# Pooling pass: where ScalarE's joining copy of two widths stands in its queue

## The chip, the cores and the metric

One core of a Trainium2 chip runs the whole program. The metric is device time in microseconds (us) of one execution; lower is better. The core's engines run side by side, each through its own list of instructions in the order in which it was written: PE multiplies matrices into banks of PSUM, DVE (VectorE) and ACT (ScalarE) do element-wise work and copy results out of the banks, POOL (GpSimd) does a little more of the same, and SP issues the DMA transfers. They wait for one another on semaphores.

## What is computed

A token encoder layer: normalise, one input projection, three mixers side by side (A: a gated MLP over chunks of 128 positions, B: pooling, C: a Fourier transform), each with a SiLU gate, one output projection, and a normalised residual. The change is in mixer B, which cuts to this:

```python
POOL_WINDOWS = (2, 4, 8, 16)
for g, w in enumerate(POOL_WINDOWS):          # four groups of 96 channels
    lo = jnp.clip(pos - w // 2, 0, s)
    hi = jnp.clip(pos + w // 2, 0, s)
    mean = (cs[:, hi] - cs[:, lo]) / (hi - lo)  # cs: running sum over positions
    outs.append(mean - zf[..., sl])
yb = mixer_b(b_in, b_w, b_scale) * jax.nn.silu(b_gate)
```

The inputs are two sequences of 4096 and 2048 positions, 1024 channels wide, in fp32.

## The kernel before

The kernel goes through the 6144 positions several times. The pass that matters here (about 485 to 950 us of the execution) computes mixer B's input z and its gate g for six blocks of 1024 positions; a pass of the same form for mixer A follows it. Each block is two halves h = 0, 1 of 512 positions (TB), and 384 channels are three tiles t = 0, 1, 2 of 128 rows. Because four pooling widths of 96 channels lie on three tiles of 128 rows, every tile holds rows of two widths.

**Products and slots.** Each block's projection is done with seven products instead of eight (a Strassen-like scheme), in the order P1, X1, P2, X2, Y1, X3, Y2 (`WIDE["b"]`). One product is one `slot` call. A slot runs its product three times, once for each t (twelve groups of matmuls of 128x512, three for each of four k, L141 to L143, 36 in all), and between them come the other engines' steps: `fill_a` before the copy out of the first bank, `fill_b` before the second, then `beside()`, which does one step of the Fourier mixer. The third bank's copy is put off to the start of the next slot (`tail`). Also at the start of a slot the operand of the next product is cut into a high part (ACT, L137) and a low part (DVE, L138). P1, X1, X2 and X3 accumulate in one bank per tile: P1 is copied out (ACT, L1337, into z), X1's matmuls then add onto the same bank, which is copied out again (L1339), and so on. So X1's first matmul on tile t waits until P1's copy of tile t is done. X2 (L1343) and X3 (L1347) are copied out by ACT too; P2 (L1341), Y1 (L1345) and Y2 (L1349) are added out by DVE.

**Pooling.** `pool_means` takes one tile of z and forms sums of 2, 4, 8, 16 neighbours by adding shifted slices on DVE (L1230 to L1243): tile 0 ends in `b` on rows 96 up, tile 1 in `b` on all rows, tile 2 in `c`. The last addition writes the wider window's rows into `a`; the rows of the narrower window are joined into `a` by one ACT copy, `nc.scalar.copy(a[rows, to], src[rows, to])` (L1245). Then, after the first `yield`, DVE scales and subtracts z on all rows (L1250). `sums(h, t)` runs a tile up to the first yield, `means(h, t)` the rest. `silu(h)` is three ACT activations (L1289), each followed by a copy of 8 columns; `gate(h)` is three DVE products (L1311) and puts three stores on the list for SP.

**Where the six joins of a block stand.** The slots' lists `fa` (fill_a) and `fb` (fill_b) say it: (0,0) in slot X2's fill_a, (0,1) in its fill_b, (0,2) in Y1's fill_a, (1,0) in Y2's fill_a, (1,1) in its fill_b, and (1,2) in fill_a of the next block's P1, where the next block's `new_z` (three copies of 16 columns, L1276) comes ahead of it and `means(1,1)` and `silu(0)` behind it. The last block's (1,2) stands in the same place of the first slot of mixer A's pass, whose P1 is copied out by ACT at L1483. `close_sequence` runs `pool_means` with n = 8 for the end of a sequence. All this is under a hand-written schedule: each engine runs its instructions in the order in which the program writes them.

Of the kernel before, what the change touches and what calls it, by code (L numbers as in the profile page):

```python
# [18 lines left out]
TB = 512  # L19
# [14 lines left out]
def hybrid_encoder(  # L34
# [33 lines left out]
    nc = tc.nc  # L68
# [209 lines left out]
    def ftile(name, shape, dt=F32):  # L278
        return fpool.tile(list(shape), dt, tag="f", name=name, bufs=7)
# [50 lines left out]
    def add_rest(sq, eng):  # L330
        eng.tensor_add(sq[0], sq[0], sq[2])
        eng.tensor_add(sq[0][:, 0:HB], sq[0][:, 0:HB], sq[0][:, HB : 2 * HB])
        return sq[0]

    def sum_rows(name, halves):

        n = 2 * len(halves)
        ps = bank(f"pss{name}", (P, NCH))[:, :n]
        for c in range(n):
            lh = halves[c // 2][:, (c % 2) * P : (c % 2) * P + P]  # L340
            nc.tensor.matmul(ps[:, c : c + 1], lh, ones[:, 0:1], start=True, stop=True)
        return ps
# [276 lines left out]
    with tc.manual_schedule(engines={E.PE, E.DVE, E.Activation, E.Pool}):  # L619
# [3 lines left out]
        rows = sum_rows("00", [add_rest(sqa, V)])  # L623
# [28 lines left out]
        rows = sum_rows("01", [add_rest(sqb, V)])  # L652
# [168 lines left out]
    def load_operand(j):  # L821
        if j < len(todo):
            n, b, m = todo[j]
            lo = lp[j % 3].tile([P, 2, 4, HB], F32R, tag="l", name=f"{n}{b}_{m}l")
            for h in range(2):
                nc.sync.dma_start(
                    lo[:, h].bitcast(F32).rearrange("p k t -> p (k t)"), op_d[2 * b + h, OUT_ORDER.index(m)]
                )
            whole[j] = lo

    def cut_operand(j):

        if j < len(todo):
            n, b, m = todo[j]
            lo = whole.pop(j)
            hi = hp[j % 2].tile([P, 2, 4, HB], F32R, tag="h", name=f"{n}{b}_{m}h")
            for h in range(2):
                split(lo[:, h].bitcast(F32), hi[:, h], lo[:, h])
            cut[j] = hi, lo
# [26 lines left out]
    def part(i, what):  # L866
        if 0 <= i < len(steps) and getattr(steps[i], what):
            getattr(steps[i], what)()

    def beside():  # L870
        i = at[0]
        if i <= len(steps) + 1:
            part(i - 2, "store")
            part(i + 2, "load")
            part(i, "compute")
            part(i + 2, "pre")
            at[0] += 1
# [279 lines left out]
            steps.extend(transform_steps(s, pair))  # L1157


    stores, tail = [], []  # L1160

    def flush(lst):
        fs, lst[:] = lst[:], []
        for f in fs:
            f()

    def slot(j, pairs, evict, fill_a=(), fill_b=(), loads=(), then=None, cuts=(), late=False, fill_c=(), more=0):


        m = todo[j][2]  # L1170
        load_operand(j + 2)
        if not late:
            flush(stores)
        for f in loads:
            f()
        flush(tail)
        cut_operand(j + 1)
        op = cut.pop(j)
        ps = pairs[0].product(m, op)
        for f in fill_a:  # L1180
            f()
        evict(0, ps)
        if late:
            done, stores[:] = stores[:late], stores[late:]
            flush(done)
        beside()
        ps = pairs[1].product(m, op)
        for f in cuts:
            f()
        for f in fill_b:  # L1190
            f()
        evict(1, ps)
        beside()
        for f in fill_c:
            f()
        last = pairs[2].product(m, op)
        for _ in range(more):
            beside()
        if then:
            then()  # L1200
        tail.append(lambda: evict(2, last))
# [17 lines left out]
    def pool_means(z, n, t, name, corr_at=None):  # L1219


        V = nc.vector

        def tile_(x, tag, bufs):
            if n < TB:
                return ftile(f"p{x}{name}", (P, n + 16))
            return e1.tile([P, TB + 16], F32, tag=tag, name=f"p{x}{name}", bufs=bufs)

        a, b = tile_("a", "a", 6), tile_("b", "w", 2)
        V.tensor_add(a[:, 1 : n + 16], z[:, 0 : n + 15], z[:, 1 : n + 16])  # L1230
        to = slice(8, n + 8)
        if t == 0:
            V.tensor_add(b[96:, to], a[96:, 7 : n + 7], a[96:, 9 : n + 9])  # L1233
            rows, src = slice(96, P), b
        else:
            V.tensor_add(b[:, 2 : n + 15], a[:, 1 : n + 14], a[:, 3 : n + 16])
            if t == 1:
                V.tensor_add(a[64:, to], b[64:, 6 : n + 6], b[64:, 10 : n + 10])
                rows, src = slice(0, 64), b
            else:  # L1240
                c = tile_("c", "w", 2)
                V.tensor_add(c[:, 4 : n + 13], b[:, 2 : n + 11], b[:, 6 : n + 15])
                V.tensor_add(a[0:96, to], c[0:96, 4 : n + 4], c[0:96, 12 : n + 12])  # L1243
                rows, src = slice(96, P), c
        nc.scalar.copy(a[rows, to], src[rows, to])  # L1245
        yield a
        if corr_at is not None:
            k, src = corr_at
            V.tensor_mul(a[:, k : k + 8], a[:, k : k + 8], corr_sb[:, 16 * t + src : 16 * t + src + 8])
        V.scalar_tensor_tensor(a[:, to], a[:, to], invw[t], z[:, to], ALU.mult, ALU.subtract)  # L1250
        yield a

    class PoolBlock:
# [41 lines left out]
        def sums(self, h, t):  # L1295
            self.half[h, t] = pool_means(
                self.z[h][t], TB, t, f"{self.b}_{h}_{t}", (16, 0) if self.t0 == 0 and h == 0 else None
            )
            next(self.half[h, t])
# [34 lines left out]
        def evict(self, m, t, ps):  # L1334
            z, g = self.z, self.g
            if m == "P1":
                nc.scalar.copy(z[0][t][:, 16:], ps)  # L1337
            elif m == "X1":
                nc.scalar.copy(g[0][t][:, 8:], ps)  # L1339
            elif m == "P2":  # L1340
                nc.vector.tensor_add(z[0][t][:, 16:], ps, z[0][t][:, 16:])  # L1341
            elif m == "X2":
                nc.scalar.copy(g[1][t][:, 8:], ps)  # L1343
            elif m == "Y1":
                nc.vector.tensor_add(g[1][t][:, 8:], ps, g[1][t][:, 8:])  # L1345
            elif m == "X3":
                nc.scalar.copy(z[1][t][:, 16:], ps)  # L1347
            else:
                nc.vector.tensor_add(g[0][t][:, 8:], ps, g[0][t][:, 8:])  # L1349

    before = None
    for b in range(NB // 2):
        blk = PoolBlock(b)
        pairs = [Wide(t, f"b{b}_{t}") for t in range(3)]
        p = before
        means = lambda who, h, t: lambda: who.means(h, t)
        sums = lambda who, h, t: lambda: who.sums(h, t)
        fa = {
            0: [lambda: blk.new_z(0)], 1: [lambda: blk.new_g(0)], 2: [],
            3: [lambda: blk.new_g(1), sums(blk, 0, 0)], 4: [sums(blk, 0, 2), means(blk, 0, 1)],  # L1360
            5: [lambda: blk.new_z(1), lambda: blk.silu(1)], 6: [blk.keep_ends, sums(blk, 1, 0)],
        }
        fb = {i: [] for i in range(7)}
        fb[3], fb[6] = ([sums(blk, h, 1), means(blk, h, 0)] for h in range(2))
        fb[4] = [means(blk, 0, 2)]
        if p:
            fa[0] += [lambda: p.sums(1, 2), lambda: p.means(1, 1), lambda: p.silu(0)]
            fb[0] += [lambda: p.means(1, 2), lambda: p.gate(0)]
            fa[1] += [lambda: p.gate(1)]
            fa[2] += [p.close_sequence]  # L1370
        for i, m in enumerate(WIDE["b"]):
            cuts, loads = [], []
            if b == 0 and i < 5:
                cuts.append(lambda i=i: cut_wide_weights(WIDE["b"][i + 2]))
            if b == NB // 2 - 1 and i > 0:
                loads.append(lambda i=i: load_wide_weights("a", WIDE["b"][i - 1]))
                if i > 1:
                    cuts.append(lambda i=i: cut_wide_weights(WIDE["b"][i - 2]))
            slot(7 * b + i, pairs, lambda t, ps, m=m, blk=blk: blk.evict(m, t, ps), fa[i], fb[i], loads, None, cuts, 3, (), 1 if b > 3 and i < 6 or b == 3 and i in (1, 2, 4, 5) else 0)
        before = blk  # L1380
# [197 lines left out]
    for b in range(NB // 2):  # L1578
# [53 lines left out]
        for i, m in enumerate(WIDE["a"]):  # L1632
            ev = lambda t, ps, m=m, blk=blk: blk.evict(m, t, ps)
            j = 7 * (b + NB // 2) + i
            slot(j, pairs, ev, fa[i], fb[i], ld[i], then.get(i), ct[i], False, fc[i], 1 if i in (3, 5) else 0)
# [23 lines left out]
    for q in range(NS):  # L1659
# [21 lines left out]
        for i, m in enumerate(OUT_ORDER):  # L1681
# [40 lines left out]
            if q < NS - 1:  # L1722
                if m in ("X3", "Y2"):
                    c = 1 if m == "X3" else 0
                    rr = rstd(c)
                    for j, hs in ((0, h0), (1, h1)):
                        src = ps["P"] if (c == 0 and j == 0) else cc[c][:, hs]
# [169 lines left out]
```

## Time and profile before

| | us |
|---|---|
| median of 3 runs | 1843.7 |
| lowest and highest of them | 1839.59, 1850.41 |
| the profiled execution, its time | 1844.26 |
| its span in the trace | 1842.5 |

The profile is of one execution. A time in it counts from the start of the span. A row of a timeline gives start, duration, engine, line, operation, the tiles written and read, how many instructions were merged, and in brackets how long the engine had been idle before it and what ended that. Where a tile's name ends in h or l, it is the high or low part of an operand; zb is z, gb the gate, pa, pb and pc the three work tiles of `pool_means`, Ab the bank of P1, X1, X2, X3.

### The profile page before, as it was taken

How to read it: one execution, taken by the hardware profiler on the slowest of the kernel's cores; microseconds unless marked ns; L12 is line 12 of the kernel's file. 1: busy time of each engine (PE TensorE's matmuls, PEld its weight loads, DVE VectorE, ACT ScalarE, POOL GpSimd, SP SyncE). 2: the span in 40 equal slices, each digit the busy share in tenths (PEclk: the TensorE clock that was granted, in tenths of full speed). 3: DMA queues.
4: the chain of work that ended last, by engine and by line, in shares of the span. 5: the costliest groups of instructions: out<-in, count | busy, mean ns of one | idle time of the engine just before them, and what ended most of it. 6: DMA issues, size and time to landing. Idle time of an engine off the chain costs nothing. (4 is left out here: it accounts for less than half of the span.)

```text
span 1842.5 us, 27621 instructions
## 1 busy us (share of the span) xinstructions
PE 1737.2 (94%) x9784; PEld 1498.0 (81%) x9784; DVE 1386.5 (75%) x2320; ACT 915.9 (50%) x1766; POOL 427.5 (23%) x293
## 2 busy tenths in 40 slices
PE   5999999999998989799889999999989999999998
PEld 4999999999877777688677888778867888888886
DVE  8877777898588887667766677667776777777786
ACT  4766664335454554445545665646663433434332
POOL 5001121231000000000010100100115566665664
PEclk9999999999999999999899999999989999999999
DMA  6999997786868886879687577665934454454543
GB/s 248 324 335 342 350 358 273 278 309 250 281 227 272 279 306 246 275 273 306 231 291 266 198 241 255 221 219 168 310 124 161 161 170 162 160 170 162 171 149 114
DMA packets 221146, 443.83 MB, mean 241 GB/s; under 512 B 29776, under 2 KB 112336, under 8 KB 221008
## 3 DMA queue, kind: packets, MB, share of 16 engines
q1 hardware_dynamic: 221008, 442.07, 69.8%
q8 instruction: 77, 1.26, 0.3%
q14 instruction: 61, 0.50, 0.1%
HBM read 297.81 MB, written 150.47 MB: 243 GB/s over the span
## 5 line engine op out<-in xcount | busy, mean ns | idle before, releaser
L1421 POOL TENSOR_TENSOR lnst<-lnst,mhalf 128x16 f32<-128x16 f32 x12 | 38.2, 3180 | 525.5 <-DVE lnst L1420 289.2
L1729 POOL TENSOR_TENSOR cc<-cc,xr 128x1024 f32<-128x1024 f32 x46 | 110.3, 2398 | 53.5 <-DVE cc L1728 53.5
L398 DVE SCALAR_TENSOR_TENSOR xp<-xp,g_sb,rbc 128x256 f32<-128x256 f32 x192 | 97.5, 574 | 4.7 <-ACT rbc L382 3.2
L1432 ACT ACTIVATE vn<-vn,lnst 128x96 f32<-128x96 f32 x192 | 71.0, 456 | 43.7 <-DVE lnst L1427 42.5
L1670 ACT ACTIVATE junk<-cc 128x512 f32<-128x512 f32 x72 | 45.5, 632 | 86.0 <-DVE cc L1711 49.9
L137 ACT CAST yo_X<-y 128x512 fp32r<-128x512 f32 x60 | 34.9, 620 | 91.5 <-PE Xo L143 75.5
L138 DVE TENSOR_TENSOR yo_P<-y,yo_P 128x512 fp32r<-128x512 f32 x48 | 70.0, 1458 | 7.6 <-ACT yo_P L137 7.4
L1274 POOL MEMSET zb<- 128x16 f32 x6 | 0.5, 111 | 315.6 <-ACT zb L1272 254.3
L353 POOL TENSOR_TENSOR rr<-ssq,mhalf 128x4 f32<-128x4 f32 (+1 forms) x13 | 17.8, 1370 | 205.4 <-DVE ssq L351 118.5
L1728 DVE SCALAR_TENSOR_TENSOR cc<-cc,orr,pgb 128x512 f32<-128x512 f32 x69 | 53.8, 807 | 15.2 <-POOL orr L1678 15.2
L365 ACT ACTIVATE xrow<-xrow 128x512 f32<-128x512 f32 x88 | 54.9, 627 | 20.9 <-DMA xrow<-in_x_sample 20.0
L138 DVE TENSOR_TENSOR yo_X<-y,yo_X 128x512 fp32r<-128x512 f32 x48 | 58.9, 1226 | 0.2
L137 ACT CAST yo_P<-y 128x512 fp32r<-128x512 f32 x48 | 29.4, 615 | 47.1 <-PE Xo L143 26.1
L177 DVE TENSOR_TENSOR ys<-y,y 128x512 f32<-128x512 f32 x24 | 24.6, 1028 | 33.1 <-DMA y<-yc_d 32.9
L1417 DVE BATCH_NORM_STATS2 lnst<-vn 128x6 f32<-128x96 f32 x192 | 44.2, 230 | 6.3 <-ACT vn L1432 6.0
L1670 ACT ACTIVATE junk<-Po 128x512 f32<-128x512 f32 x24 | 14.4, 599 | 68.1 <-PE Po L143 68.1
L141 PE MATMUL pd<-mt,o 128*128 128x256 f32 (+1 forms) x80 | 27.0, 338 | 21.6 <-DMA mt<-const_m 18.6
L141 PE MATMUL Ab<-b_X1h,wbX1h 128*128 128x512 f32 x72 | 32.0, 444 | 15.7 <-ACT zb L1337 12.0
L1678 POOL TENSOR_TENSOR orr<-oms,mhalf 128x1 f32<-128x1 f32 x48 | 27.0, 563 | 84.1 <-DVE oms L1676 84.1
L1245 ACT COPY pa<-pb 32x512 f32<-32x512 f32 (+1 forms) x24 | 14.8, 619 | 56.6 <-DVE pb L1233 32.2
L1441 PE MATMUL pm<-ws,vn 128*32 128x128 f32 x1152 | 39.9, 290 | 2.8 <-ACT vn L1432 2.8
L1441 PEld LDWEIGHTS pm<-ws,vn 128*32 128x32 f32 x1152 | 34.6, 117 | 8.4 <-ACT vn L1432 5.5
(742 smaller groups left out, 6730.4 us busy)
## 6 DMA issues: line engine op xcount, KB each, us to landing
op_d<-xp SPq DMA_DIRECT2D x72, 512.0 KB, 5.1
mt<-const_m SPq DMA_DIRECT2D x56, 512.0 KB, 7.0
xp<-in_xt SPq DMA_DIRECT2D x48, 512.0 KB, 6.0
out<-cc SPq DMA_DIRECT2D x46, 512.0 KB, 2.9
xr<-in_x_sample SPq DMA_DIRECT2D x32, 512.0 KB, 4.3
xrow<-in_x_sample SPq DMA_DIRECT2D x28, 512.0 KB, 5.7
o<-o_d SPq DMA_DIRECT2D x40, 256.0 KB, 6.4
vn_d<-vg SPq DMA_DIRECT2D x48, 192.0 KB, 4.0
```

The costliest lines, as they stand in the source:

```text
L137: last_cast[0] = nc.scalar.copy(hi, src)
L138: return (nc.gpsimd if pool_lo else nc.vector).tensor_sub(lo, src, hi.bitcast(F32))
L141: nc.tensor.matmul(ps, lh, rh, start=first, stop=False, skip_group_check=True)
L365: nc.scalar.activation(half, half, AF.Square, accum_out=ss[:, 2 * c + h : 2 * c + h + 1])
L398: nc.vector.scalar_tensor_tensor(xs[q][:, sl], xs[q][:, sl], g8_sb[:, 4 * kh + k : 4 * kh + k + 1], rbc[a], ALU.mult, ALU.mult,)
L1417: nc.vector.bn_stats(st[:, j], self.v[h][c][:, 96 * hd : 96 * hd + 96])
L1421: nc.gpsimd.tensor_tensor(rv, va, mhalf, ALU.pow)
L1432: nc.scalar.activation(v_, v_, AF.Identity, bias=nb[:, j : j + 1], scale=rv[:, j : j + 1])
L1441: nc.tensor.matmul(pm[32 * hd : 32 * hd + 32, c * P : (c + 1) * P], self.v[h][c][:, 96 * hd + 32 * t : 96 * hd + 32 * t + 32], ws[:, hd], ...
L1670: nc.scalar.activation(junk, src, AF.Square, accum_out=ss[:, j : j + 1])
L1728: nc.vector.scalar_tensor_tensor(cc[c][:, hs], src, rr, pgb[:, hs], ALU.mult, ALU.mult)
L1729: nc.gpsimd.tensor_add(cc[c], cc[c], xr[c])
```

## The change

`pool_means` no longer writes the joining copy at once. It puts it on a list, `joins`, and `slot` writes what is on the list right after each `evict`, the copy or addition out of a bank: once after the first bank's and once after the second's. For n < TB (the ends of a sequence) the list is emptied at once, so those six small joins stay where they were.

```diff
-    stores, tail = [], []
+    stores, tail, joins = [], [], []
...
         for f in fill_a:
             f()
         evict(0, ps)
+        flush(joins)
         if late:
...
         for f in fill_b:
             f()
         evict(1, ps)
+        flush(joins)
         beside()
...
-        nc.scalar.copy(a[rows, to], src[rows, to])
+        joins.append(lambda: nc.scalar.copy(a[rows, to], src[rows, to]))
+        if n < TB:
+            flush(joins)
         yield a
```

## Rows read from the trace of the kernel before

**Rows 1.** Page, head and part 1: busy time, share of span, instructions

```profile
span 1842.5 us, 27621 instructions
PE 1737.2 (94%) x9784; PEld 1498.0 (81%) x9784; DVE 1386.5 (75%) x2320; ACT 915.9 (50%) x1766; POOL 427.5 (23%) x293
```

**Rows 2.** PE's waits, 505 to 960 us: total, times, longest

```profile
PE pd L141 <- DMA mt<-const_m: 14.4, 4, 8.3
PE Ab L141 <- ACT zb L1337: 12.0, 3, 6.8
```

**Rows 3.** Timeline of all engines, 612 to 636 us: P1 and X1, third block

```profile
614.77 0.39 PE L141 MATMUL Ab<-b_P1h,wbP1h 128*128 128x512 f32 x1
...
618.61 0.41 ACT L1276 COPY zb<-edge 128x16 f32<-128x16 f32 x3
...
622.70 0.39 PE L143 MATMUL Ab<-b_P1h,wbP1l 128*128 128x512 f32 x1
...
623.26 0.61 ACT L1245 COPY pa<-pc 32x512 f32<-32x512 f32 x1 [4.24 <-DVE pc L1242]
...
626.19 1.55 ACT L1337 COPY zb<-Ab 128x512 f32<-128x512 f32 x3
626.82 0.29 PEld L141 LDWEIGHTS Ab<-b_X1h,wbX1h 128*128 128x128 f32 x1 [4.15 <-ACT zb L1337]
626.82 0.80 PE L141 MATMUL Ab<-b_X1h,wbX1h 128*128 128x512 f32 x1 [3.73 <-DMA b_X2l<-op_d]
...
629.87 0.39 PE L142 MATMUL Ab<-b_X1l,wbX1h 128*128 128x512 f32 x1
```

**Rows 4.** Timeline of all engines, 548 to 572 us: the same, second block

```profile
555.21 0.41 ACT L1276 COPY zb<-edge 128x16 f32<-128x16 f32 x3
...
558.07 0.39 PE L143 MATMUL Ab<-b_P1h,wbP1l 128*128 128x512 f32 x1
...
559.85 0.61 ACT L1245 COPY pa<-pc 32x512 f32<-32x512 f32 x1 [4.24 <-DVE pc L1242]
...
563.40 0.80 PE L141 MATMUL Ab<-b_X1h,wbX1h 128*128 128x512 f32 x1 [4.95 <-ACT zb L1337]
...
566.57 0.58 ACT L1337 COPY zb<-Ab 128x512 f32<-128x512 f32 x1
...
568.12 2.36 DVE L138 TENSOR_TENSOR b_P2l<-b_P2l,b_P2h 128x1024 fp32r<-128x1024 f32 x2 [0.31 <-ACT b_P2h L137]
...
568.52 0.40 PE L141 MATMUL Ab<-b_X1h,wbX1h 128*128 128x512 f32 x1
```

**Rows 5.** Timelines of ACT and PE, 675 to 700 us: the same, fourth block

```profile
684.15 0.41 ACT L1276 COPY zb<-edge 128x16 f32<-128x16 f32 x3
...
685.17 0.39 PE L143 MATMUL Ab<-b_P1h,wbP1l 128*128 128x512 f32 x1
692.34 0.80 PE L141 MATMUL Ab<-b_X1h,wbX1h 128*128 128x512 f32 x1 [6.78 <-ACT zb L1337]
...
698.04 0.39 PE L142 MATMUL Ab<-b_X1l,wbX1h 128*128 128x512 f32 x1
```

**Rows 6.** Timelines of PE and SP, 900 to 936 us: mixer A's first slots

```profile
916.21 0.60 PE L141 MATMUL Aa<-a_X1h,waX1h 128*128 128x512 f32 x1 [3.10 <-ACT s1a L1483]
...
920.61 3.37 SPq L1318 DMA_DIRECT2D yb_d<-pa  x6
...
932.96 0.47 PE L141 MATMUL pd<-mt,o 128*128 128x512 f32 x1 [2.63 <-DMA mt<-const_m]
```

**Rows 7.** Timelines of DVE and SP, 692 to 768 us: fourth block's P2, a table load

```profile
711.63 0.69 DVE L1341 TENSOR_TENSOR zb<-Pb,zb 128x512 f32<-128x512 f32 x1 [2.03 <-PE Pb L143]
...
745.90 0.64 SPq L1015 DMA_DIRECT2D mt<-const_m  x1
```

**Rows 8.** Windows (length, busy by engine, PE clock, DMA share, GB/s): one block, one peak

```profile
563.40:626.80 63.40, 59.69 (x252) 48.88 (x252) 54.27 (x90) 32.80 (x63) 0.00 (x0) 0.96 0.88 300
616.00:620.00 4.00, 4.00 (x20) 3.30 (x19) 3.93 (x7) 2.83 (x6) 0.00 (x0) 1.00 1.05 405
```

## Prediction

> **What bounds the kernel now.** I read the head of the page first: PE is busy for 94% of the span, and no other engine for more than 75% [rows 1]. The kernel can only get faster where PE stands still or runs at its low clock, so the second view is who PE waits for in the pooling pass. Two waits lead the list: 14.4 us for DMA loads of a table of the Fourier steps, and 12.0 us for P1's copy out of its bank, in three waits [rows 2]. The third view is the timeline around such waits, and there the reader is to follow one chain backwards. In the third block PE ends P1 at 622.70, where a next matmul could start 0.23 us later, but X1 starts at 626.82 [rows 3]. PE's row names a DMA there, the weight load of the same moment names P1's copy; X1 reads nothing of that DMA's tile (it is X2's operand), so I count this as a wait for the copy too. ACT's copy of P1 ran at 626.19, although its product had been finished since about 617.5 (first matmul at 614.77, twelve at 0.227 us each, the spacing of the 36 of P1: (622.70 - 614.77) / 35). What held it is the join: ACT had finished its small copies at 618.61 + 0.41 = 619.02 and stood still for 4.24 us until DVE had the sum `pc` for it, at 623.26; then came the silus, then P1's copy [rows 3]. The same picture stands in the second block [rows 4], in the fourth [rows 5] and, with 3.10 us, at the seam to mixer A's pass [rows 6]. In the fifth block there is no such wait, in the sixth one of 12.0 - 4.95 - 6.78 = 0.27 us [rows 2, 4, 5].
>
> Each stop costs a second time. After it X1's matmuls come 0.436 us apart instead of 0.227: (629.87 - 626.82) / 7 in the third block. That is the lower of PE's two clock levels, 1.2 against 2.4 GHz. Seven slow steps cost 3.05 - 1.59 = 1.46 us there [rows 3], twelve cost 5.12 - 2.72 = 2.40 in the second block [rows 4], thirteen cost 5.70 - 2.95 = 2.75 in the fourth [rows 5].
>
> **What the change moves.** It removes and adds no work: 36 large joins of about 0.61 us [rows 3, 4] stay. They issue no DMA, and none passes anything on SP's or POOL's queue. By the lists of the slots, half of them don't move at all: in Y1 and Y2 the next `evict` is DVE's, so ACT's order is the same. Two per block pass one X2 copy each. Nobody waits for that copy early (the bank is next used two slots later); at most X3's cut starts one copy (0.58 us [rows 4]) earlier. I cost these twelve at nothing; PE's lead covers them, and without it they would be worth up to 0.6 us a block, either way. What counts is (1,2): six joins that now stand behind `silu(0)` and P1's first copy.
>
> ACT then goes from its small copies straight into the silus, which took 626.19 - (623.26 + 0.61) = 2.32 us, and P1's copy, 0.58 [rows 3, 4]. The silus need the Y2 addition of the gate, which in the code's order is ahead of the sums on DVE, so they find their input. DVE's chain doesn't change: the join still starts when `pc` is done, if ACT is through with P1's copy by then. Site by site:
>
> Third block: copy done at 619.02 + 2.32 + 0.58 = 621.92, before PE is free at 622.93. The whole 626.82 - 622.93 = 3.89 us and the 1.46 of slow clock go: 5.35 us. The second and third copies follow the join at 623.87, at 624.5 and 625.1, ahead of X1's need for them at 622.93 + 2.72 and + 5.44 [rows 3].
>
> Second block: copy done at 555.62 + 2.90 = 558.52, PE free at 558.30. X1 starts with 0.22 us of wait instead of 5.10 [rows 4]. But here a new wait takes over. The third copy stays where it is, ending at 567.15, since two casts of a Fourier step, fed by DVE, are ahead of it on ACT, and X1 wants its third bank at 558.52 + 5.44 = 563.96. PE stands 3.19 us in mid-X1. X1's end was 563.40 + 36 x 0.227 + 2.40 = 573.97. Now it is 567.15 + 2.72 = 569.87 at full clock, with P2's low operand ready at 570.48 [rows 4], so 3.5 us of gain at most; a slow restart like the 1.46 us after 3.73 us idle [rows 3] leaves 2.6. I take 2.6 (a stop of 3.19 is close to that row); ends 2.0 and 3.5.
>
> Fourth block: copy done at 684.56 + 2.90 = 687.46, PE free at 685.40: 2.06 us of wait instead of 6.94, 4.88 gained [rows 5]. Of the 2.75 for the clock nothing or all may go. The row with a shorter stop, 2.63 us, has its first matmul at 0.47 us against 0.80 after the long stops [rows 4 to 6]. I take half, 6.3 in all; ends 4.9 and 7.6.
>
> Fifth block nothing, sixth 0.3. The seam to mixer A: at most the 3.10 us [rows 6], for PE's next stop there is for a table whose load stands on SP behind six stores at 920.61, and these wait for DVE's gates, which come behind a weight cast on ACT and its low part on DVE. That chain moves by less than P1's copy does. I take 2.5; ends 0 and 3.1.
>
> Sum: 5.35 + 2.6 + 6.3 + 0.3 + 2.5 = 17.0 us, ends 3.9 + 2.0 + 4.9 + 0 + 0 = 10.8 and 5.35 + 3.5 + 7.6 + 0.3 + 3.1 = 19.9.
>
> **Does it survive to the end?** After each site the next late thing could be DVE. In the third block DVE is busy for 54.27 of 63.40 us [rows 8]; what it does from P2's last addition on starts when PE ends P2 (DVE idle 2.03 us there, released by PE, [rows 7]), so an earlier X1 pulls that chain forward with it. The transfers: that block moves 300 GB/s x 63.4 us = 19.0 MB, and the 4 us around 618 show 405 GB/s [rows 8], at which it would need 47 us. The block keeps some 59, so I see room. The Trainium skill, "DMA: Bandwidth & Descriptors", section "Where 436 GB/s comes from", speaks more against the change: the HBM side limits such transfers to about 358 GB/s per core. By it the block would need 53 us, my estimate, still under 59, so the sum would be the same; the 405 GB/s of the trace is above that limit, and the measurement decides.
>
> Against the profiled execution's 1844.26 us this is 1827.3. That execution lies 0.6 us above the median of three, which run from 1839.6 to 1850.4, so I put the forecast at 1827, with a range of its own of 1821 to 1835.
>
> **Rivals.** (a) Absorbed at the table load. In the fourth block PE stops for 8.3 us for a table [rows 2] whose load SP issues at 745.90 [rows 7]. If that were tied to DMA and not to PE, it would swallow all of the three sites before it, 14.2 us, and leave 2.8: 1841. Against it: the load stands in SP's order behind stores of results that DVE computes after P2's addition at 711.63, which PE released [rows 7].
>
> (b) It doesn't do what it says: half of the joins can't move, and should PE in truth wait for something that lands together with P1's copy (the row that names the DMA, [rows 3]), the rest would be worth nothing either: 1843. Against it are the waits that name the copy alone [rows 2, 4, 5].
>
> (c) Slower, by the second and third copies. They stay behind the join and behind whatever `beside()` puts on ACT. If both end later than 2.72 and 5.44 us after the first, PE stops twice inside X1, and all 36 matmuls run at the low clock. With two stops of 3.2 us as in the second block and 36 x (0.436 - 0.227) = 7.5 us, an X1 costs 13.9 us more than its bare time, where today's three sites cost 7.5, 5.35 and 9.7: 41.7 - 22.6 = 19 us more, 1863. It decides at 625.65 in the third block, where the second copy should end at 624.5 [rows 3]; one such stop in the second block is in my sum already. The Trainium skill, "PSUM — Partial Sum Buffer", section "Engine vs sequencer instructions", says that ScalarE's queue is strictly first in, first out, so neither copy could pass a late join. The trace agrees as far as it shows: ACT idle for 4.24 us with P1's finished bank behind the join [rows 3].
>
> (d) Better: both disputed clock losses vanish and X3's earlier cut counts: 22 to 27 us less, 1817 to 1822.
>
> **How the numbers follow.** Forecast 0.76, (a) 0.09, (b) 0.06, (c) 0.05, (d) 0.04. The range 1818 to 1839 holds the forecast's bounds and most of (d), and leaves (a), (b) and (c) out, 0.20. A measurement here tells 0.5%, 9.2 us, from no change, so below 1834.5 is faster: nearly all of the forecast and (d), 0.77; (a), (b) and the forecast's weak end 0.18; (c) 0.05.
>
> **What would show it.** In the profile after, ACT's order at a block's start is small copies, silus, one P1 copy, join, P1 copy. PE's waits for L1337 shrink from 12.0 us (15.7 with the third block's) to some 5.5: 2.1 in the fourth block, and 3.2 in the second, now before X1's 25th matmul instead of its first. The idle time of ACT before the joins from `pc` falls in the moved six; DVE's rows keep their order. Wrong would be: X1 starting no earlier (another wait behind the copy), the table's wait grown by what the sites gained (a), or new stops inside X1 of the third and fourth blocks (c).

## The result and the profile after

| | median, us | beside it, before | ratio, 95% interval |
|---|---|---|---|
| changed kernel | 1818.16 | 1843.62 | 0.9872 [0.9846, 0.9899] |
| the same again, on another chip | 1817.21 | 1841.72 | 0.9866 [0.9841, 0.9890] |

The kernel became faster by 23.6 us on the first chip (18.6 to 28.4 by the interval) and 24.7 on the second; 17 had been forecast. The profiled execution of the changed kernel took 1819.41 us, with a span of 1817.6 instead of 1842.5. The page's head and busy times, beside [rows 1]:

```profile
span 1817.6 us, 27618 instructions
PE 1727.3 (95%) x9784; PEld 1489.1 (82%) x9784; DVE 1385.4 (76%) x2320; ACT 916.6 (50%) x1766; POOL 430.3 (24%) x293
```

ACT and DVE do the same work as before (916.6 and 1385.4 us against 915.9 and 1386.5); what shrank is PE's idle time and its time at the low clock. An edit moves the lines behind it, so L1337 of the kernel before is L1341 here and has other numbers in some of the runs below. Who PE waits for in the pooling pass (485 to 945 us; total, times, longest), beside [rows 2]:

```profile
PE pd L141 <- DMA mt<-const_m: 14.4, 4, 7.0
...
PE Ab L141 <- ACT zb L1341: 3.0, 1, 3.0
PE pmx L141 <- DVE gm L1121: 2.7, 1, 2.7
```

The waits that name P1's copy fell from 12.0 us in three to 3.0 us in one, to which 1.20 us in the fourth block come that a row puts down to a DMA (see there); some 5.5 had been forecast. The four table waits stayed at 14.4. The third block, timelines of ACT and PE, beside [rows 3]:

```profile
615.05 0.41 ACT L1280 COPY zb<-edge 128x16 f32<-128x16 f32 x3
...
617.66 0.58 ACT L1341 COPY zb<-Ab 128x512 f32<-128x512 f32 x1
619.69 0.61 ACT L1247 COPY pa<-pc 32x512 f32<-32x512 f32 x1 [1.45 <-DVE pc L1244]
620.33 1.08 ACT L1341 COPY zb<-Ab 128x512 f32<-128x512 f32 x2
619.61 0.39 PE L143 MATMUL Ab<-b_P1h,wbP1l 128*128 128x512 f32 x1
619.84 0.39 PE L141 MATMUL Ab<-b_X1h,wbX1h 128*128 128x512 f32 x1
```

ACT's order is now small copies, silus, one P1 copy, join, P1 copies. The first copy ends at 618.24, 1.6 us before PE is through with P1, and X1 starts 0.23 us after P1's last matmul. ACT still stands 1.45 us for `pc`, but nobody stands behind it. Second block, timelines of ACT and PE, beside [rows 4]:

```profile
555.85 0.58 ACT L1341 COPY zb<-Ab 128x512 f32<-128x512 f32 x1
557.89 0.62 ACT L1247 COPY pa<-pc 32x512 f32<-32x512 f32 x1 [1.46 <-DVE pc L1244]
...
563.17 0.62 ACT L137 CAST fh<-fo 128x512 fp32r<-128x512 f32 x1 [4.05 <-DVE fo L948]
564.09 0.62 ACT L137 CAST fh<-fo 128x512 fp32r<-128x512 f32 x1 [0.31 <-DMA yb_d<-pa]
564.62 0.58 ACT L1341 COPY zb<-Ab 128x512 f32<-128x512 f32 x1
556.12 0.39 PE L143 MATMUL Ab<-b_P1h,wbP1l 128*128 128x512 f32 x1
556.49 0.50 PE L141 MATMUL Ab<-b_X1h,wbX1h 128*128 128x512 f32 x1
...
565.25 0.80 PE L141 MATMUL Ab<-b_X1h,wbX1h 128*128 128x512 f32 x1 [3.00 <-ACT zb L1341]
```

X1 starts at once, and PE then stops for 3.00 us inside it: the third copy is behind the two casts of the Fourier step, and these wait 4.05 us for DVE. The fourth block, timelines of ACT and PE, beside [rows 5], and in the last line the table stop that follows it in slot Y2:

```profile
677.69 0.58 ACT L1341 COPY zb<-Ab 128x512 f32<-128x512 f32 x1
676.73 0.39 PE L143 MATMUL Ab<-b_P1h,wbP1l 128*128 128x512 f32 x1
678.32 0.50 PE L141 MATMUL Ab<-b_X1h,wbX1h 128*128 128x512 f32 x1 [1.20 <-DMA zz_d<-fz]
...
733.80 0.77 PE L141 MATMUL pd<-mt,o 128*128 128x512 f32 x1 [7.03 <-DMA mt<-const_m]
```

PE goes on 0.05 us after the copy's end (677.69 + 0.58 = 678.27), whatever DMA its row names, and 6.78 us of wait have become 1.20. The seam to mixer A, PE's timeline, beside [rows 6]:

```profile
894.10 0.39 PE L143 MATMUL Aa<-a_P1h,waP1l 128*128 128x512 f32 x1
...
911.67 0.47 PE L141 MATMUL pd<-mt,o 128*128 128x512 f32 x1 [4.32 <-DMA mt<-const_m]
```

X1 starts at 894.33, right behind P1; before, PE stood there for 3.10 us. The next stop, for a table, grew from 2.63 to 4.32 us.

**Where the time went.** Each trace gives the start of the first matmul of every P1. The gain of a block is the shrinkage of the distance from one P1 to the next; the seam is the distance from mixer A's first P1 to its first X2. Every column is one execution. In the first block nothing was edited in the columns "block-start joins alone", "fourth block alone" and "silu first", and it differs there by -0.42 to +1.44 us: a single cell is no surer than that.

| gain, us | forecast | changed | the same again | block-start joins alone | X2 joins alone | fourth block alone | silu first, no change |
|---|---|---|---|---|---|---|---|
| first block | 0 | 0.71 | 0.72 | -0.24 | -0.68 | -0.42 | 1.44 |
| second | 2.6 | 1.15 | 2.42 | 1.15 | 0.43 | -0.38 | 2.96 |
| third | 5.35 | 5.35 | 5.35 | 5.35 | 0.45 | -0.24 | 1.67 |
| fourth | 6.3 | 9.66 | 7.58 | 6.43 | 0.75 | 6.83 | 2.29 |
| fifth | 0 | -0.27 | -0.13 | -0.69 | 0.46 | -0.03 | -2.92 |
| sixth | 0.3 | 0.79 | 0.80 | 0.33 | 1.65 | 0.33 | 0.13 |
| seam | 2.5 | 2.66 | 2.49 | 2.64 | 0.06 | 0.12 | 2.24 |
| sum | 17.0 | 20.05 | 19.23 | 14.97 | 3.12 | 6.21 | 7.82 |

The spans differ by 24.9 us and, in the run of the same kernel again, by 22.9. What the sums leave lies ahead of the pass (1.2 and 2.6 us) and behind the seam, where the kernels are the same; it is taken up below.

### The profile page after: what moved, and what is told of

The parts are those of the page before. It is cut to its first block, busy times and chain, and to the rows that moved or that the text cites. A ratio compares the mean times of both kernels' runs of the same rounds, so it can differ in the third digit from the quotient of the medians.

```text
span 1817.6 us, 27618 instructions
## 1 busy us (share of the span) xinstructions
PE 1727.3 (95%) x9784; PEld 1489.1 (82%) x9784; DVE 1385.4 (76%) x2320; ACT 916.6 (50%) x1766; POOL 430.3 (24%) x293
## 5 line engine op out<-in xcount | busy, mean ns | idle before, releaser
L138 DVE TENSOR_TENSOR yo_X<-y,yo_X 128x512 fp32r<-128x512 f32 x48 | 59.3, 1236 | 0.5 <-ACT yo_X L137 0.3
L1674 ACT ACTIVATE junk<-Po 128x512 f32<-128x512 f32 x24 | 14.4, 599 | 69.2 <-PE Po L143 69.2
L141 PE MATMUL pd<-mt,o 128*128 128x256 f32 (+1 forms) x80 | 27.1, 338 | 21.3 <-DMA mt<-const_m 18.3
L1422 DVE BATCH_NORM_AGGREGATE lnst<-lnst 128x2 f32<-128x6 f32 x192 | 34.9, 182 | 6.6
L191 POOL TENSOR_TENSOR y<-y,y 128x512 f32<-128x512 f32 x23 | 31.9, 1388 | 33.0 <-DVE yo_X L138 29.3
```

Of the source, the lines that this page charges most:

```text
L138: return (nc.gpsimd if pool_lo else nc.vector).tensor_sub(lo, src, hi.bitcast(F32))
L141: nc.tensor.matmul(ps, lh, rh, start=first, stop=False, skip_group_check=True)
L1674: nc.scalar.activation(junk, src, AF.Square, accum_out=ss[:, j : j + 1])
```

## The experiments

The first four were compared on one chip with a before of 1842.48 us. The runs with the Fourier step held, with the loads first, with both, and the second run of the changed kernel were compared on another, with 1841.72; the run with the table first and the second run with the loads first on a third, with 1844.3.

**Only the joins at a block's start.** `pool_means` gets a flag, and only the (1,2) joins are put off.

```diff
+        joins.append(lambda: nc.scalar.copy(a[rows, to], src[rows, to]))
+        if not put_off:
+            flush(joins)
...
+                (h, t) == (1, 2),
```

> Only the joins of (1,2), the six that stand at the seam from one block to the next, go behind P1's first copy; the others are written at once, as before. Theory (the gain is X1's earlier start at the seams, nothing else): 1820 us, at most 2 us behind the changed kernel's 1818, with X1 starting early in the second, third and fourth block as there. Rival (the twelve joins that pass an X2 copy carry a large share, through an earlier cut of X3's operand): 1828 us or more.

1822.81 us, ratio 0.9900 [0.9863, 0.9937]. By the times alone this is a gain of 11.6 to 25.2 us, which holds the theory's 1820 as well as the rival's 1828; the trace decides. X1 starts as in the changed kernel in the second, third and fourth block and at the seam, and the pass gains 14.97 us. So the six block-start joins carry some 15 of the 19 to 20 us of the pass. Two stops that the changed kernel doesn't have, or has shorter, stay (PE's timeline):

```profile
539.96 0.50 PE L142 MATMUL Yb<-b_Y2l,wbY2h 128*128 128x512 f32 x1 [1.43 <-DVE b_Y2l L138]
...
868.92 0.77 PE L141 MATMUL pmx<-th,cmh 128*128 128x512 f32 x1 [3.97 <-DVE gm L1121]
```

**Only the joins of slot X2.** The same flag, set for (0,0) and (0,1).

```diff
+                (h, t) in ((0, 0), (0, 1)),
```

> Only the joins of (0,0) and (0,1) go behind the X2 copies; (1,2) stays where it was. Theory: 1842 us, 0 to 2 us under the kernel before, and PE's waits for P1's copy as before (12.0 us by the copy's name). Rival (X2's joins carry a large share): 1834 us or less.

1838.48 us, ratio 0.9983 [0.9966, 1.0000]: a gain of 0 to 6.3 us, half way between the theory's 1842 and the rival's 1834. The three waits for P1's copy stand as they were. PE's waits, 485 to 945 us:

```profile
PE Ab L141 <- ACT zb L1342: 12.0, 3, 6.8
...
PE pmx L141 <- DVE gm L1121: 2.5, 1, 2.5
```

But two stops are shorter, the two that the run before this one left alone. The stop for Y2's low part in the first block is 1.44, 1.43, 1.43 and 1.43 us in before, in the run with the block-start joins alone, in the one of the fourth block alone and in silu first. In all eight runs in which these joins moved it is 0.35 or 0.36. The stop for `gm` in the sixth block is 3.68, 3.97, 3.36 and 3.58 us in the former, and 2.24 to 2.89 in the eight. So the twelve joins that I had costed at nothing are worth about 1.1 + 1.0 us of stops, and what slow clock follows them. The 3.12 us that the table gives the whole pass are more than these stops, and less sure: they lie within what single executions differ by. The two stops in the kernel before, PE's timeline:

```profile
542.07 0.50 PE L142 MATMUL Yb<-b_Y2l,wbY2h 128*128 128x512 f32 x1 [1.44 <-DVE b_Y2l L138]
...
883.88 0.77 PE L141 MATMUL pmx<-th,cmh 128*128 128x512 f32 x1 [3.68 <-DVE gm L1121]
```

How an earlier X2 copy reaches Y2's low part, three slots on, the timelines of ACT and DVE show link by link (516 to 543 us), first before, then with the X2 joins alone:

```profile
516.00 2.00 ACT L137 CAST b_Y1h<-b_Y1l 128x1024 fp32r<-128x1024 f32 x2 [4.33 <-PE Pb L143]
522.06 1.48 ACT L855 CAST wbX3h<-wbX3l 128x1536 fp32r<-128x1536 f32 x1
528.21 2.00 ACT L137 CAST b_X3h<-b_X3l 128x1024 fp32r<-128x1024 f32 x2
539.66 2.35 DVE L138 TENSOR_TENSOR b_Y2l<-b_Y2l,b_Y2h 128x1024 fp32r<-128x1024 f32 x2
```

```profile
518.08 2.00 ACT L137 CAST b_Y1h<-b_Y1l 128x1024 fp32r<-128x1024 f32 x2 [4.33 <-PE Pb L143]
523.53 1.48 ACT L855 CAST wbX3h<-wbX3l 128x1536 fp32r<-128x1536 f32 x1
529.20 2.00 ACT L137 CAST b_X3h<-b_X3l 128x1024 fp32r<-128x1024 f32 x2
540.66 2.35 DVE L138 TENSOR_TENSOR b_Y2l<-b_Y2l,b_Y2h 128x1024 fp32r<-128x1024 f32 x2
```

Counted from the cast of Y1's operand (2.08 us later in the second trace), the cast of X3's weights starts 0.61 us earlier, the cast of X3's operand 1.09 and Y2's low part 1.08. Before, ACT ran the join, then the X2 copy that had long been ready, then the cast. With the order exchanged the copy runs while the join still waits for DVE, and the cast follows the join at once. DVE's next low part and pooling sums follow that cast, and the next join follows those sums, so two copies of 0.58 us or so add up. Nobody waited for the X2 copy; what waited stood behind it. In the sixth block DVE's addition into `gm` (L1121) comes 1.08 us earlier in the same way, from 26.14 to 25.06 us behind the cast of Y1's operand.

**The fourth block alone.** Of all joins only the one at the fourth block's start.

```diff
+                (h, t) == (1, 2) and self.b == 2,
```

> Only one join of the 36 is moved, (1,2) at the seam to the fourth block. Theory: X1 of that block starts some 5 us earlier without a slow restart, P2 some 8 us earlier, and this is kept to the end: 1836 us. Rival (the table load a block later is tied to DMA and swallows it): the stop of 8.3 us at that load grows to about 16, and the time stays at 1843.

1833.71 us, ratio 0.9964 [0.9944, 0.9984]: 1836 lies in it, 1843 doesn't. PE's timeline, the start of X1 and the table stop:

```profile
686.34 0.50 PE L141 MATMUL Ab<-b_X1h,wbX1h 128*128 128x512 f32 x1 [1.97 <-ACT zb L1342]
...
744.21 0.76 PE L141 MATMUL pd<-mt,o 128*128 128x512 f32 x1 [5.44 <-DMA mt<-const_m]
```

The wait fell to 1.97 us, and the table stop didn't grow: it is 5.44 us where before had 8.29. The gain stays to the end of the pass (6.21 us there): rival (a) falls. One part of the theory missed: a slow restart did follow the stop, ten steps and 1.7 us, so P2 came 5.85 us earlier in its block and not 8.

**The old place of the join, and silu ahead of the sums.** The kernel before, with `silu(0)` written ahead of `sums(1,2)`: the join doesn't stand in front of the silus any more, but still in front of P1's first copy. The cut shows the blocks' place; at the seam to mixer A `silu(0)` is moved to the front likewise.

```diff
-             fa[0] += [lambda: p.sums(1, 2), lambda: p.means(1, 1), lambda: p.silu(0)]
+             fa[0] += [lambda: p.silu(0), lambda: p.sums(1, 2), lambda: p.means(1, 1)]
```

> The join stays ahead of P1's copy, but silu of the previous block's first half is written ahead of the sums, so only the silus leave ACT's stretch between the join and P1's copy. Theory (X1 starts when P1's copy ends, and that now ends 0.58 us after the join): a wait of PE of 2.7 us in the second block, 1.5 in the third, 4.6 in the fourth, 0.9 at the seam to mixer A; about half of the gain, 1831 us. Rival (the silus were the whole of it, the join's own place nothing): 1819 us. Rival (the join's place is the whole of it): 1843 us.

1830.88 us, ratio 0.9939 [0.9915, 0.9964]. PE's timeline, X1's start in the second, third and fourth block:

```profile
556.08 0.60 PE L141 MATMUL Ab<-b_X1h,wbX1h 128*128 128x512 f32 x1 [2.65 <-ACT zb L1337]
...
616.90 0.50 PE L141 MATMUL Ab<-b_X1h,wbX1h 128*128 128x512 f32 x1 [1.80 <-ACT zb L1337]
...
680.02 0.80 PE L141 MATMUL Ab<-b_X1h,wbX1h 128*128 128x512 f32 x1 [4.12 <-ACT zb L1337]
```

The waits were 4.95, 3.73 and 6.78 us before: 2.30, 1.93 and 2.66 us are off, on the mean the 2.3 us of the silus, and the rest stays, at 0.83 us at the seam as well. So the join in front of the copy holds PE, and the silus behind it added their own time; the time lies where the theory had it, and 1819 and 1843 lie outside the interval. Here the third block's row names the copy too, and not the DMA of before, so rival (b) falls with it.

**The second block's Fourier step behind the third copy.** The changed kernel, with the second of that one slot's two `beside()` held until the next operand has been cut, which puts P1's third copy ahead of the two casts.

```diff
-        beside()
+        if hold:
+            held.append(1)
+        else:
+            beside()
```

> The changed kernel, and in the second block's P1 slot the Fourier step that stands between the second and the third product is written after the next slot's operand cut, so that its two casts are no longer ahead of P1's third copy on ScalarE, nor its sums ahead of P2's operand on VectorE. Theory (in the changed kernel the third copy, held by those casts, stops PE 3.2 us inside X1, and 14 slow matmuls follow): the stop goes, P2 of the second block starts 5 to 6 us earlier, 1813 us. Rival (VectorE holds P2's operand back anyway): the stop only moves to P2's first matmuls, 1817 us.

1821.88 us, ratio 0.9892 [0.9869, 0.9914], neither the theory's 1813 nor the rival's 1817. The stop inside X1 went, as the theory said: X1 to P2 took 8.36 us instead of 14.05, and P2 began 5.7 us earlier in its block than in the changed kernel (7.2 earlier than in before). Yet the block as a whole gained 2.36 us, no more than the repetition of the changed kernel (2.42). The timelines of ACT and SP and the window of 567 to 593.5 us (length, busy by engine, clock, DMA share, GB/s) show where it was given back; the last fence has the same load in the changed kernel, SP's timeline:

```profile
579.33 1.05 ACT L137 CAST b_Y1h<-b_Y1l 128x1024 fp32r<-128x1024 f32 x1 [6.51 <-DMA b_Y1l<-op_d]
571.75 2.35 SPq L939 DMA_DIRECT2D fz<-z_d  x4
574.14 0.90 SPq L826 DMA_DIRECT2D b_Y1l<-op_d  x2
567.00:593.50 26.50, 24.77 (x109) 20.01 (x107) 20.81 (x37) 12.82 (x21) 0.00 (x0) 1.00 1.00 349
```

```profile
570.73 0.90 SPq L826 DMA_DIRECT2D b_Y1l<-op_d  x2
```

Y1's operand lands late, and ACT stands 6.51 us for it, DVE behind ACT. SP's timeline names what held it. Its load stands right behind four loads of the Fourier step (571.75 + 2.35 = 574.10), and these behind stores of the step that was held. Counted from P1's start, it was issued 23.78 us into the block, where the changed kernel has 22.54, although P2 began so much earlier. Its two parts then landed in 5.1 and 6.5 us, no slower than there (6.4 and 7.2). X3's operand is not late by its load: it had landed by about 586.4, and ACT came to its cast at 591.49, behind a join that waited for DVE. PE's stop for X3 was 1.77 us. So moving the step on ACT's queue moved its transfers on SP's too, and those hold the next operand; no run moved that load alone. The DMA engines are busy for the whole stretch, at 349 GB/s; in the changed kernel the same stretch shows 0.86 and 294 GB/s, in its repetition 0.93 and 317. The Trainium skill, "DMA: Bandwidth & Descriptors", section "Where 436 GB/s comes from", puts the limit of such transfers at about 358 GB/s per core. These 26.5 us come near it, the 4 us at 405 GB/s [rows 8] stand above it; whether it is the limit here no run shows.

**The Fourier loads ahead of the stores.** The changed kernel again, with two lines of `beside()` exchanged, to see whether the table stop comes from SP's order.

```diff
-            part(i - 2, "store")
             part(i + 2, "load")
+            part(i - 2, "store")
```

> The changed kernel, with the loads of a Fourier step written ahead of the stores of an earlier one, where before the stores came first. The first table loads then don't stand behind the last fold's six stores, which wait for VectorE. Theory (the stop of 7 to 8 us at the first table load comes from SP's order behind VectorE's fold results, not from the transfers' rate): that stop shrinks to 2 us or less, 1811 us. Rival (the stop is tied to the transfers themselves): the stop stays at 7 us and the time at 1818.

1815.92 us, ratio 0.9855 [0.9833, 0.9878], and once more, on the third chip, 1817.15, 0.9869 [0.9841, 0.9897]:

> The kernel with the Fourier loads ahead of the stores once more, unchanged, on the same chip as the run with the table first: by theory R the two agree within 0.3%, by rival Q the one with the table first is 5 to 7 us faster. Its stop for the table should be about 6.7 us again.

The intervals hold the changed kernel's ratio; time and stop are those of the rival. SP's and PE's timelines of the first of the two, and SP's waits (700 to 735 us):

```profile
724.64 0.62 SPq L1012 DMA_DIRECT2D o<-o_d  x1
725.30 0.62 SPq L1015 DMA_DIRECT2D mt<-const_m  x1
...
730.64 0.80 PE L141 MATMUL pd<-mt,o 128*128 128x512 f32 x1 [6.71 <-DMA mt<-const_m]
SPq L1012 <- DVE fz L955: 11.5, 1, 11.5
```

The table now stands ahead of the stores, and comes no earlier for it. SP waits for 11.5 us in front of the load of `o`, the table's partner, until DVE has made the fold's last addition (L955): that load can't go before it, and the table stands behind it. The stop stayed at 6.71 us (6.41 in the second run), against 7.03 and 7.70 in the changed kernel. So the theory was right that SP's order holds the table, and wrong about the place in it that does; the rival's numbers came without its reason.

**Both of the last two edits.**

> Both edits on the changed kernel: the Fourier step of the second block's P1 slot later, and loads ahead of stores. Theory (the two stops are at different places and the gains add): 1806 us. Rival (one takes what the other frees): 1811 us.

1820.09 us, ratio 0.9879 [0.9855, 0.9903], with neither 1806 nor 1811 in it: the two don't add up to anything. The second block gains 0.89 us; the table stop is 5.86 us.

**The table ahead of its operand.** The kernel with the loads first, and in each load `mt` now issued before `o`.

```diff
         def load(r, es):
-            if 0 in es:
-                ops[r] = ftile(f"o{nm}{r}", (P, 2, 2, P), F32R)
-                nc.sync.dma_start(ops[r].bitcast(F32), o_d[s][L][r][:, :, :, pair])
             if wide:
...
+            if 0 in es:
+                ops[r] = ftile(f"o{nm}{r}", (P, 2, 2, P), F32R)
+                nc.sync.dma_start(ops[r].bitcast(F32), o_d[s][L][r][:, :, :, pair])
```

> The changed kernel with the Fourier loads written ahead of the stores, as in the run before with that edit, and in each of these loads the table (mt) now ahead of the operand (o). It asks what makes the fourth block's stop of 6.7 us for the table: in the run with the loads first SP stood for 11.5 us in front of the operand's load, until DVE's last addition of the fold (L955) had been done, since the operand takes a tile that the fold uses until then; the table's load stood behind it. Theory R (the tile): the table is issued right behind the load of P1's operand, some 15 us earlier, but PE's stop stays within 1.5 us of 6.7 and is now put down to o, whose load still can't be issued ahead of L955 and took 7.4 us from issue to landing; the time stays at 1816, within 0.3%. Rival Q (the table's own 512 KB, or its place behind the operand): the stop shrinks to under 3 us, and with the slow clock behind it the time falls by 5 to 7 us, to about 1810.

1818.73 us, ratio 0.9862 [0.9833, 0.9891]. SP's and PE's timelines and SP's waits (690 to 745 us):

```profile
707.83 0.35 SPq L1012 DMA_DIRECT2D mt<-const_m  x1
723.59 0.62 SPq L1020 DMA_DIRECT2D o<-o_d  x1
...
727.08 0.80 PE L141 MATMUL pd<-mt,o 128*128 128x512 f32 x1 [4.20 <-DMA o<-o_d]
SPq L1020 <- DVE fz L955: 12.3, 1, 12.3
```

The table left 16 us earlier, and PE still stopped for 4.20 us, now for `o`, issued as late as ever (59.3 us behind the block's first matmul, against 59.5 in the run beside it). Of the 6.41 us that the run beside it had, 2.2 went with the table's later issue; the rest is the operand's load behind DVE's fold. So neither expectation held alone: the stop lies below theory R's 5.2 and above rival Q's 3, though the time, and the name in the row, are R's. The load of `o` takes a tile from the ring that the fold uses (`ftile`), which would explain why it waits for L955; a tile of its own wasn't tried. The time didn't change clear of the noise, and no kernel here is clearly faster than the changed one.

**The changed kernel once more.**

> The changed kernel once more, unchanged, for a second profile of it and more times. If the 5 us that its first profile gained in mixer A's pass, where nothing was edited, come from the change, they stand here again; if they come from how long PE's clock stays low after stops that both kernels have, they don't. Time by either: 1815 to 1823 us.

1817.21 us, ratio 0.9866 [0.9841, 0.9890]. Its X1 stops, PE's timeline, second and fourth block:

```profile
563.87 0.80 PE L141 MATMUL Ab<-b_X1h,wbX1h 128*128 128x512 f32 x1 [3.02 <-ACT zb L1341]
...
676.55 0.50 PE L141 MATMUL Ab<-b_X1h,wbX1h 128*128 128x512 f32 x1 [2.09 <-ACT zb L1341]
```

The second block's stop is the same to 0.02 us as in the first execution (3.00), the fourth's is not (1.20).

## Why the prediction was right, and where it was short

**Right: the mechanism, and that it survives.** P1's copy behind the join was what PE waited for (the joins at a block's start alone; silu first). ACT's new order, the stops that go, and the new one inside the second block's X1 came as written.

**Luck: that the time lies in the range.** 1818.16 is 0.16 us above its lower bound, the repetition's 1817.21 is below it, and both are below the 1821 that the forecast had for itself. The pass gave 20.05 and 19.23 us, about the sum's upper end, and with these alone the time would be about 1823. The other 3.5 to 5.5 us lie where I forecast nothing.

**Third block: exact.** 5.35 us forecast, 5.35 measured in three runs. The copy needed to end before PE was free, and did so by 1.6 us.

**Second block: stop exact, clock not.** The new stop is 3.16 us from the end of one matmul's spacing to the start of the next (3.19 forecast). The gain was 1.15 us in one execution and 2.42 in the other, where I had 2.6 with 2.0 as the low end. The term that was mis-sized is the slow restart: I took 1.46 us from a row with seven slow steps [rows 3]. The repetition had eight, 1.6 us; the first execution had 14, 14 x 0.209 = 2.9 us, some of them in P2. The difference to 1.46 is the whole miss in both.

**Fourth block: too low.** 6.3 forecast, with 7.6 as the high end. X1 and what follows it up to P2 gave 8.19 and 7.33 us. I had halved the 2.75 us of slow clock; all of it went in both executions, with one slow step behind the stop. The stop itself, forecast 2.06, was 1.36 and 2.25 by the same count as above. The block as a whole gained 9.66 and 7.58; in the first execution the rest is in the table stop and ahead of X3. That the slow clock went is no rule: with the fourth block alone, after a stop of 2.13, it stayed.

**Seam: the path named, the number by luck.** 2.5 forecast, 2.66 and 2.49 measured. The table stop behind it took part of the gain back, as named. But the sum took at most the 3.10 us of the stop and left out the slow clock behind it: X1 lost 3.26 us of stop and 1.71 of slow clock, 4.97 in all, and the table stop took 2.3 and 2.5 back, not 0.6. Two errors cancelled.

**The step that failed: twelve joins at nothing.** I argued that nobody waits early for an X2 copy, and that PE's lead covers what moves. The first is true and beside the point: what stands behind the copy is waited for, through ACT and DVE in turn, and the two copies of a block add up to 1.08 us, more than the "up to 0.6 us a block, either way" that I had seen and left out of the sum. PE's lead covers it in most blocks, but not at Y2 in the first and at `gm` in the sixth: there the stops shrank by 1.1 and 1.0 us (the run with these joins alone, and all others in which they moved). Before's 1.4 us wait for Y2's low part stood in the profile at 542.07, in the slots behind these joins, and I didn't ask what it hung on.

**Two rows that I misread.** The stretch of [rows 8] that I called the third block runs from the second block's X1 to the third's, and the idle 2.03 us of DVE [rows 7] are the fourth block's. The argument that an earlier X1 pulls DVE's chain forward came out all the same: the third block kept its whole 5.35 us.

**The rivals.** (a) falls with the fourth block alone and with the tables' 14.4 us, which did not grow. (b) falls with silu first. (c) falls in the third block: both later copies are done at 621.41, and PE wants the second bank at 619.84 + 2.72 = 622.56. (d) gave the time that came, but only part of its conditions: the fourth block's clock loss vanished, the second's did not. X3's earlier cut did count, as a link on the way to Y2's, for 1.1 us.

**What stays open.** In the pass 20.05 and 19.23 us are accounted for; the ratios say 23.6 [18.6, 28.4] and 24.7 [20.3, 29.3] us. The first interval holds the pass's number and the second nearly does, so it isn't shown that the rest is more than scatter. The remaining 3.5 to 5.5 lie ahead of the pass, where nothing was changed, and in mixer A's pass and the last stage. In the first execution mixer A's pass after the seam gains another 5 us (from 21.3 to 26.4); in the repetition, from its first X2 to its last Y2, only 1.6 (21.8 to 23.4), and the runs with the fourth block or the X2 joins alone gain 4.6 and 2.4 there. The edits don't order these numbers, so I take them for differences of single executions; that isn't shown. Nor did I follow the table stop of the fourth block to its end: it hangs on the load of `o` behind DVE's fold, and no run gave that load its own tile.

## What to carry to other kernels

In a queue that runs in the written order, a copy that waits for another engine belongs behind the copy that frees a bank for the matmuls: the six joins at a block's start were worth some 15 us without one instruction less. Cost such a move by three clocks: when the bank's copy would now end, when PE is free, and what is next on the same queue (here the Fourier casts that held the third copy). And look for small stops downstream of the moves that seem idle, and ask what stands behind the moved copy, not only who waits for it; the twelve that I wrote off paid some 2 us. Last, a move on one engine's queue can carry transfers along on SP's, as the held Fourier step did.

## What the runs showed of the hardware

After a stop PE's matmuls often come 0.43 us apart for a while instead of 0.227, and how long that lasts doesn't follow from the stop. The stop of 2.99 to 3.02 us inside the second block's X1 stands at the same place in six traces. In the first execution of the changed kernel and with the block-start joins alone 14 slow steps (2.9 us) followed it, at a granted clock of 0.50 from 565.3 to 570 us of the first; in the repetition and in three other runs it was seven or eight (1.5 to 1.7 us). At the fourth block's X1, stops of 1.97 us (fourth block alone), 1.96 (block-start joins alone) and 2.23 (both of the last two edits) were followed by some 1.7 us of slow steps each, and stops of 2.09 (the repetition), 1.88 (the Fourier step held) and 1.74 (the second run with the loads first) by one slower step, 0.1 to 0.2 us. The slow steps needn't begin at once: with the block-start joins alone the first step was 0.1 us longer, the next four were normal, and only then came nine slow ones (granted clock 1.00 from 678.9 to 680 us, 0.54 from 680.3 to 684). The same stop of 3.10 us at the seam cost 1.71, 1.55 and 1.76 us in three kernels. One such restart is worth 0.1 to 2.9 us here, so a forecast can give its bounds, and not its value. The Trainium skill, "TensorE: Matmul & The Clock Gate", section "What's actually happening", says of a kernel's start that the number of cold matmuls varies from run to run of the same kernel; the 14 and 8 in two executions of the changed kernel show the same in the middle of one.
